# A mixture-of-experts kernel with a second model's context stream woven in: the order of the context's four branches

## The chip, the cores and the metric

The kernel runs on one core of a Trainium2 chip. A time is the device time of one execution in microseconds (us); the kernel before takes 1780.83 us, the median of three runs (1779.35 to 1781.1). Engines: PE (TensorE, matmuls), PEld (its weight loads), DVE (VectorE), ACT (ScalarE), POOL (GpSimd), SP (SyncE, which here only issues DMAs). Each engine works through its own instructions strictly in the order in which they were written into the program, and waits at semaphores for the others.

## The reference, cut to what matters

Two transformer blocks follow one another. The first ends in a mixture of experts: 256 tokens, 32 experts of three weight matrices each, two experts per token.

```python
def expert_block(args):
    xblk, e = args
    return (jax.nn.silu(xblk @ w1[e]) * (xblk @ w3[e])) @ w2[e]
```

The second block is a model of two layers over 256 latent tokens and 256 context tokens. In its first layer the context goes through the same four branches as the latents, then through a projection and a feed-forward part:

```python
yc_a = fourier_mix(pc[..., COL_FOURIER:COL_FOURIER + gw])
yc_b = dense_attention(heads(pc[..., COL_NA:COL_NA + gw]), na_kc, na_vc).reshape(bsz, -1, gw)
yc_c = spatial_gating(pc[..., COL_SGU:COL_SGU + 2 * gw], ...)
qc = heads(pc[..., COL_DIFF:COL_DIFF + gw])
oc_d = diff_attend(qc[..., :DIFF_QK_DIM], qc[..., DIFF_QK_DIM:], df_kc[..., :DIFF_QK_DIM], ...)
yc = jnp.concatenate([yc_a, yc_b, yc_c, yc_d], axis=-1) @ w_out[l]
cx = cx + cg1 * yc
cx = cx + cg2 * sq_relu_mlp(hc2, w_ff1[l], w_ff2[l])
```

The four branches read the same normalized context and write different columns of `yc`; none of them needs another. The context depends on nothing of the first block, so the kernel computes its first layer beside the experts.

## The kernel before, in words

**The experts.** `moe` (L1091) goes through 32 experts, e0 to e31, in groups of 4, 4, 8, 8, 8. At a group's start `gather` (L1003) picks the tokens of its experts with matmuls against a 0/1 matrix (`pm<-oh,xn`). For each expert `scatter_mat` (L1025) makes the matrix that puts results back: POOL copies `oh4`, PE transposes it (`pm<-ident,oh`, `pm<-wt,oh`). `expert` (L1040) then loads six pieces of weights, 1 MiB each (two halves of w1 and w3, two of w2), and does a chain of three matmul stages: 64 matmuls `pm<-w,xg` over w1 and w3; an eviction by ACT (`eh`) and two transposes on PE (`pm<-ident,eh`); the gated activation on ACT and DVE (`eth`, `ex`); 32 matmuls `pm<-w,ex` over w2; the weighting, split into a high and a low part (`yh`, `yl`); and 16 matmuls `acc<-yh,sc` and `acc<-yl,sc` that add the expert's result to four accumulators that stay in PSUM through all experts. Within one expert PE thus has three turns at which it waits for ACT and DVE, unless other matmuls stand in its order there: from `xg` to the transposes of `eh`, from these to `ex`, and from `ex` to `acc`.

**The side work.** The context's first layer is a Python generator, `context_side` (L1855), which calls `context_layer` (L1773), which calls `context_mixer` (L1545). Each `yield` ends a step. `moe` takes one step after each expert (`side()`, L1119; two go before e0 and one earlier still), so that step and expert stand side by side in the program. Its matmuls write `pf` tiles (two PSUM banks of their own, `ps_lin` and `ps`, L180 and L187). A linear layer is `lin` (L293): the weights (1 MiB pieces, `half`, L243) are split by ACT and DVE into a high and a low part (`wh`, `wl`), and each product takes three matmuls. Over 512 columns that is 96 matmuls with 256 moving columns (activations stationary or weights stationary by the job, `WJob`), or 48 with 512 (`TJob`). The feed-forward part, `ff_side` (L1686), has 16 steps that alternate between 96 `pf<-hh,wh` and the like (first layer) and 48 `pf<-wh,hh` and the like (second).

In `context_mixer` the steps of the kernel before are, by the expert that they follow: the neighbourhood branch (for the context a dense attention, `na`) two units each after e0 to e3; the query and key layer of the differential attention, W1, after e4; its attention, `diff`, two units each after e5 to e8, which loads no weights; W3 and the Fourier branch after e9; the gating unit (`sgu_v`, one piece w_su, `sgu`) after e10. Then `context_layer` goes on: the two halves of the output projection after e11 and e12 (`pf<-wh,yh` and the like), the norm after e13, the feed-forward part after e14 to e29.

**What sets the order.** The program's text is only the input: a scheduler with a timeline of its own puts the instructions of each engine into their final order, so that pieces of a step can stand ahead of pieces of the expert before it, and the reverse. SP's loads are ordered by it too. The 1 MiB pieces of experts and side work share ten buffers (`p16`, `p16x`): a load is issued when an earlier piece has been read. DVE, ACT and PE are shared by both streams.

Of the kernel before, what the change touches and what calls it, by code (L numbers as in the profile page):

```python
# [110 lines left out]
class Builder:  # L111
# [1433 lines left out]
    def context_mixer(self, lhs, kvc, kd_d, nlam, put):  # L1545

        W = self.a["w_in_2"][0]
        new = lambda s: self.t2([P, 2, 256], F32, s)
        nk, nv, dv, dk = kvc
        npad = self.head_pads(64)  # L1550
        self.lin(self.chunk(W[0]), 8, 512, [WJob(lhs, self.two_w(npad, nk))])
        yield
        self.lin(self.chunk(W[2]), 8, 512, [TJob(lhs, self.two_t(nv, dv))])
        yield
        yield from itertools.islice(self.in_turn(self.na(npad, [nk], [nv], None, put), 0), 1, None, 2)
        dpad = self.head_pads(32)
        self.lin(self.chunk(W[1]), 8, 512, [WJob(lhs, self.two_w(dpad, dk))])
        yield
        self.planes(dk, kd_d)
        df = self.diff(self.padded(dpad, [dk]), 2, [dv], nlam, 0, put)  # L1560
        yield from itertools.islice(self.in_turn(df, 0), 1, None, 2)
        fa, sv = new("fa"), new("sv")
        self.lin(self.chunk(W[3]), 8, 512, [TJob(lhs, self.two_t(fa, sv))])
        self.fourier(fa, put)
        yield
        self.sgu_v(sv, 0)
        su = new("su")
        self.lin(self.chunk(self.a["w_su_2"][0], (P, 2048)), 8, 256, [WJob(lhs, self.two_w(su, None))])
        self.sgu(su, sv, 0, put)
        yield  # L1570

    def mixer(self, l, lhs, kvc, kd_d, nlam, put, proj, late, w, held, fill):

# [537 lines left out]
```

## Time and profile before

| | |
|---|---|
| median of the timed runs | 1780.83 us (1779.35 to 1781.1) |
| the profiled execution | 1776.12 us, span 1774.3 us |
| PE / PEld busy | 1657.3 us (93%) / 1317.0 us (74%) |
| DVE / ACT / POOL busy | 961.2 us (54%) / 724.0 us (41%) / 61.6 us (3%) |
| DMA | 495.83 MB, mean 279 GB/s |
| the experts' weights | 192 pieces of 1 MiB, median 12.1 us from issue to landing |

The span holds one execution from its first to its last instruction; 1.8 us of the profiled execution lie around it. The experts take the stretch from some 455 us to 1073 us, in slices 11 to 25 of the page's second part. There PE and the DMA engines are both mostly at 9 tenths, so the share of the whole span says little: what a change is worth is read from the places inside the stretch where PE waits, and from what it waits for there. An idle time in square brackets in a timeline's row is that of the engine just before the row, with what ended it; "issue" means that the profile shows nothing that did.

### The profile page before, as it was taken

Reading aid. Unit: us, or ns where it says so; the run is one execution under the profiler, and the core shown is the slowest. Engines: PE = TensorE matmul, PEld = TensorE weight load, DVE = VectorE, ACT = ScalarE, POOL = GpSimd, SP = SyncE. Lnnn points to the kernel's source line nnn. Section 1 sums busy time; section 2 is a strip of 40 time slices with the busy share of each in tenths; the row PEclk is TensorE's granted clock in tenths of the full one; section 3 lists DMA queues with packets and bytes.
Section 4 is the critical chain, followed back from the end, with each engine's and each line's share of the span. In section 5 each row is a group of like instructions: output and inputs, shape, how many; then the busy total and the mean of one; then the engine's idle time right before and its main releaser. Section 6 shows DMA issues by size and latency. Waiting matters only on the chain.

```text
span 1774.3 us, 31435 instructions
## 1 busy us (share of the span) xinstructions
PE 1657.3 (93%) x13088; PEld 1317.0 (74%) x13088; DVE 961.2 (54%) x1719; ACT 724.0 (41%) x1257; POOL 61.6 (3%) x104
## 2 busy tenths in 40 slices
PE   4999999999888998999999997999999999899998
PEld 1678766667565556776677666878999998689998
DVE  5626556467223445544454457586545456766555
ACT  2414434343223433333233336565444445645443
POOL 0000000000000000000000001010000000100000
PEclk9899999999899999999999999999999999989999
DMA  9654588977699999989979997725877746245551
GB/s 372 278 211 169 199 317 310 345 278 265 240 420 420 421 395 407 379 365 420 416 318 401 421 394 268 232 81 172 291 253 264 263 165 208 76 130 188 192 190 43
DMA packets 79060, 495.83 MB, mean 279 GB/s; under 512 B 8928, under 2 KB 15744, under 8 KB 22464
## 3 DMA queue, kind: packets, MB, share of 16 engines
q1 hardware_dynamic: 74496, 478.30, 70.6%
q0 software_dynamic: 3152, 10.47, 2.0%
q10 hardware_dynamic: 1264, 4.98, 0.7%
q8 instruction: 105, 1.72, 0.4%
q14 instruction: 43, 0.35, 0.1%
HBM read 486.91 MB, written 6.82 MB: 278 GB/s over the span
## 4 chain that ended last, share of the span: by engine, by line
PE 64%; DVE 3%; DMA 3%; ACT 2%; issue 2%; POOL 0%; DVEq 0%; ACTq 0%; POOLq 0%
PE pf L200 23%; PE pm L200 19%; PE acc L200 11%; PE pa L200 5%; PE pj L200 3%; PE pm L203 1%; DMA w<-in_w_in 1%; PE pf L203 1%; DMA w<-in_e 1%; PE pada L200 1%; DVE wl L209 1%; DMA w<-in_w_out 1%; DVE sm L1337 1%; ACT e L206 0%; ACT wh L206 0%
## 5 line engine op out<-in xcount | busy, mean ns | idle before, releaser
L209 DVE TENSOR_TENSOR wl<-w,wh 128x1024 fp32r<-128x1024 f32 x346 | 422.4, 1225 | 385.4 <-PE pa L200 100.5
L206 ACT ACTIVATE wh<-w 128x1024 fp32r<-128x1024 f32 x346 | 362.8, 1059 | 407.1 <-PE pa L200 169.5
L200 PE MATMUL pf<-hh,wh 128*128 128x256 f32 x592 | 167.0, 284 | 4.6 <-ACT hh L206 2.4
L200 PE MATMUL pf<-hh,wl 128*128 128x256 f32 x592 | 164.4, 283 | 2.1 <-DVE wl L209 2.1
L200 PE MATMUL pf<-hl,wh 128*128 128x256 f32 x592 | 165.3, 281 | 0.5 <-DVE hl L209 0.5
L200 PE MATMUL acc<-hh,wh 128*128 128x256 f32 x512 | 143.5, 280 | 0.0
L200 PE MATMUL acc<-hl,wh 128*128 128x256 f32 x512 | 142.9, 279 | 0.0
L200 PE MATMUL acc<-hh,wl 128*128 128x256 f32 x512 | 142.9, 279 | 0.0
L200 PE MATMUL pm<-w,xg 128*32 128x256 f32 x2048 | 131.2, 387 | 2.7 <-ACT sm L206 1.8
L200 PEld LDWEIGHTS pf<-hh,wh 128*128 128x128 f32 x592 | 111.8, 189 | 9.8 <-ACT hh L206 3.1
L200 PEld LDWEIGHTS pf<-hh,wl 128*128 128x128 f32 x592 | 110.5, 189 | 5.0 <-DVE wl L209 2.8
L200 PEld LDWEIGHTS pf<-hl,wh 128*128 128x128 f32 x592 | 111.8, 189 | 1.5 <-DVE hl L209 0.9
L200 PEld LDWEIGHTS pm<-w,xg 128*32 128x32 f32 x2048 | 66.6, 111 | 50.9 <-issue 11.2
L200 PEld LDWEIGHTS acc<-hh,wh 128*128 128x128 f32 x512 | 96.4, 188 | 5.9 <-ACT wh L206 4.2
L200 PEld LDWEIGHTS acc<-hh,wl 128*128 128x128 f32 x512 | 96.8, 189 | 0.0
L200 PEld LDWEIGHTS acc<-hl,wh 128*128 128x128 f32 x512 | 96.4, 188 | 0.0
L200 PE MATMUL pada<-w,csil 128*32 128x512 f32 x576 | 83.7, 613 | 5.6 <-DMA w<-in_ada_w 5.6
L200 PE MATMUL pm<-w,ex 128*32 128x256 f32 x1024 | 63.6, 388 | 24.0 <-issue 22.3
L200 PE MATMUL pm<-hh,wh 128*128 128x256 f32 x256 | 71.7, 280 | 0.0
L200 PE MATMUL pm<-hl,wh 128*128 128x256 f32 x256 | 71.7, 280 | 0.0
L200 PE MATMUL pm<-hh,wl 128*128 128x256 f32 x256 | 71.5, 279 | 0.0
L200 PEld LDWEIGHTS pm<-w,ex 128*32 128x32 f32 x1024 | 33.8, 111 | 46.6 <-issue 28.9
(512 smaller groups left out, 3484.7 us busy)
## 6 DMA issues: line engine op xcount, KB each, us to landing
w<-in_e SPq DMA_DIRECT2D x192, 1024.0 KB, 12.1
w<-in_ff SPq DMA_DIRECT2D x96, 1024.0 KB, 5.6
w<-in_ada_w SPq DMA_DIRECT2D x72, 1024.0 KB, 7.1
w<-in_w_in SPq DMA_DIRECT2D x54, 1024.0 KB, 7.8
w<-in_w_out SPq DMA_DIRECT2D x16, 1024.0 KB, 7.0
w<-in_ret_w_o SPq DMA_DIRECT2D x4, 1024.0 KB, 5.2
w<-in_w_su SPq DMA_DIRECT2D x3, 1024.0 KB, 6.5
adab<-in_ada_b SPq DMA_DIRECT2D x9, 256.0 KB, 12.6
```

What stands on the lines that cost most here:

```text
L200: return self.nc.tensor.matmul(out, lhsT, rhs, start=start, stop=stop, skip_group_check=True)
L203: return self.nc.tensor.transpose(out, in_, self.ident)
L206: return self.nc.scalar.activation(out, in_, f, **k)
L209: return self.nc.vector.tensor_tensor(out, a, b, op=op)
L1337: self.nc.vector.tensor_reduce(mn, s, AX.X, ALU.min)
```

## The change

Within `context_mixer` two blocks of lines change places: W3, the Fourier branch and the gating unit now come straight after the neighbourhood branch, and the differential attention comes last. No instruction's operands change in size, and the number of steps stays 13.

```diff
         yield from itertools.islice(self.in_turn(self.na(npad, [nk], [nv], None, put), 0), 1, None, 2)
-        dpad = self.head_pads(32)
-        self.lin(self.chunk(W[1]), 8, 512, [WJob(lhs, self.two_w(dpad, dk))])
-        yield
-        self.planes(dk, kd_d)
-        df = self.diff(self.padded(dpad, [dk]), 2, [dv], nlam, 0, put)
-        yield from itertools.islice(self.in_turn(df, 0), 1, None, 2)
         fa, sv = new("fa"), new("sv")
         self.lin(self.chunk(W[3]), 8, 512, [TJob(lhs, self.two_t(fa, sv))])
         self.fourier(fa, put)
...
         self.sgu(su, sv, 0, put)
         yield
+        dpad = self.head_pads(32)
+        self.lin(self.chunk(W[1]), 8, 512, [WJob(lhs, self.two_w(dpad, dk))])
+        yield
+        self.planes(dk, kd_d)
+        df = self.diff(self.padded(dpad, [dk]), 2, [dv], nlam, 0, put)
+        yield from itertools.islice(self.in_turn(df, 0), 1, None, 2)
```

By steps: W3 with Fourier now follows e4 (was e9), the gating unit e5 (was e10), W1 e6 (was e4), and the differential attention e7 to e10 (was e5 to e8). From e11 on each step follows the same expert as before. The scheduler's order moves beyond that: it differs on PE, DVE and ACT from e4 up to e30, as the three places below show.

First place: PE where W1's linear layer begins (`hh` and `hl` are the normalized context there, `wh` and `wl` the split weights). Before, it follows at once on e4's transposes (`eh_4571`) and w2 stage (`ex`):

```order
L203 MATMUL pm_4573<-ident_81,eh_4571 128x128 x2
L200 MATMUL pm_4581<-w_4534,ex_862_4577 32x256 x8
L200 MATMUL pm_4581<-w_4536,ex_862_4577 32x256 x8
L200 MATMUL pf_4628<-hh_2818,wh_4630 128x256
L200 MATMUL pf_4628<-hl_2819,wh_4630 128x256
L200 MATMUL pf_4629<-hh_2818,wh_4630 128x256
L200 MATMUL pf_4629<-hl_2819,wh_4630 128x256
```

Now it stands behind the whole of e7's first stage (`xg` into `pm_5196`, its last two rows here) and the gating unit's matmuls (`sguw,sv`):

```order
L200 MATMUL pm_5196<-w_5188,xg_4488 32x256 x2
L200 MATMUL pm_5196<-w_5190,xg_4488 32x256 x2
L200 MATMUL pf_4924<-sguw_4919,sv_4621 64x128 x8
L200 MATMUL pf_5050<-hh_2818,wh_5052 128x256
L200 MATMUL pf_5050<-hl_2819,wh_5052 128x256
L200 MATMUL pf_5050<-hh_2818,wl_5053 128x256
L200 MATMUL pf_5050<-hh_2818,wh_5052 128x256
```

W1's step follows e6 in the program's text now, but its matmuls stand behind the next expert's first stage; before, they stood ahead of it.

Second place: PE at expert e15, in the feed-forward part (`pm_6736` is e15's first stage, `eh_6769` its eviction, `hh` and `hl` the hidden rows of the side work). Before, two side matmuls stand between `xg` and the transposes, and ten (six of them here) between the transposes and `ex`:

```order
L200 MATMUL pm_6736<-w_6730,xg_5270 32x256 x2
L200 MATMUL pf_6822<-wh_6824,hh_6583 128x512
L200 MATMUL pf_6823<-wh_6824,hh_6583 128x512
L203 MATMUL pm_6771<-ident_81,eh_6769 128x128 x2
L200 MATMUL pf_6822<-wl_6825,hh_6583 128x512
L200 MATMUL pf_6822<-wh_6824,hl_6584 128x512
L200 MATMUL pf_6823<-wl_6825,hh_6583 128x512
L200 MATMUL pf_6823<-wh_6824,hl_6584 128x512
```

Now both turns have nothing in them; side matmuls come after `ex` and a gather, two ahead of `acc`:

```order
L200 MATMUL pm_6736<-w_6730,xg_5343 32x256 x2
L203 MATMUL pm_6771<-ident_81,eh_6769 128x128 x2
L200 MATMUL pm_6779<-w_6732,ex_1315_6775 32x256 x8
L200 MATMUL pm_6779<-w_6734,ex_1315_6775 32x256 x8
L200 MATMUL pm_6906<-oh_6902,xn_3197 128x256 x4
L200 MATMUL pm_6913<-oh_6902,xn_3197 128x256 x4
L200 MATMUL pf_6822<-wh_6824,hh_6583 128x512
L200 MATMUL pf_6823<-wh_6824,hh_6583 128x512
L200 MATMUL acc_3891<-yh_6798,sc_6720 128x256
```

The twelve side matmuls that filled e15's two turns have moved behind its w2 stage.

Third place: PE at expert e26 (`eh_9142`), from the transposes on. Before, 39 side matmuls (the first five here) stand between `ex` and `acc`:

```order
L203 MATMUL pm_9144<-ident_81,eh_9142 128x128 x2
L200 MATMUL pm_9152<-w_9105,ex_1724_9148 32x256 x8
L200 MATMUL pm_9152<-w_9107,ex_1724_9148 32x256 x8
L200 MATMUL pf_9197<-hh_6417,wh_9199 128x256
L200 MATMUL pf_9197<-hl_6418,wh_9199 128x256
L200 MATMUL pf_9198<-hh_6417,wh_9199 128x256
L200 MATMUL pf_9198<-hl_6418,wh_9199 128x256
L200 MATMUL pf_9197<-hh_6417,wl_9200 128x256
```

Now there are four, and the accumulation (`acc_3891`) follows them:

```order
L203 MATMUL pm_9144<-ident_81,eh_9142 128x128 x2
L200 MATMUL pm_9152<-w_9105,ex_1724_9148 32x256 x8
L200 MATMUL pm_9152<-w_9107,ex_1724_9148 32x256 x8
L200 MATMUL pf_9197<-hh_6417,wh_9199 128x256
L200 MATMUL pf_9197<-hl_6418,wh_9199 128x256
L200 MATMUL pf_9198<-hh_6417,wh_9199 128x256
L200 MATMUL pf_9198<-hl_6418,wh_9199 128x256
L200 MATMUL acc_3891<-yh_9171,sc_9093 128x256
L200 MATMUL acc_3892<-yh_9171,sc_9093 128x256
```

Here the order of the first two turns is alike in both, and the third has lost all but four of its matmuls.

## Rows read from the trace of the kernel before

**Rows 1.** Stretches: length, busy us of the engines, PEclk, DMA share, GB/s

```profile
500.00:700.00 200.00, 177.07 (x1722) 118.77 (x1713) 79.62 (x196) 67.53 (x164) 6.33 (x14) 0.98 1.01 415
640.00:700.00 60.00, 52.33 (x486) 35.31 (x478) 29.10 (x58) 18.07 (x34) 2.97 (x6) 0.97 1.01 410
700.00:1060.00 360.00, 338.81 (x3308) 255.13 (x3312) 182.59 (x285) 116.98 (x205) 8.33 (x18) 1.00 0.95 388
700.00:760.00 60.00, 59.32 (x558) 43.10 (x558) 34.49 (x65) 24.14 (x42) 1.21 (x3) 0.98 0.86 341
880.00:940.00 60.00, 55.51 (x518) 44.38 (x520) 30.03 (x42) 19.62 (x32) 0.81 (x2) 1.00 0.83 329
```

**Rows 2.** ACT's timeline (start us, us): the evictions eh of e5, e6, e8, e9, e14, e31

```profile
540.35 0.39 ACT L206 ACTIVATE eh<-pm 128x256 f32<-128x256 f32 x1
...
553.26 0.38 ACT L206 ACTIVATE eh<-pm 128x256 f32<-128x256 f32 x1 [3.71 <-PE pm L200]
...
590.72 0.39 ACT L206 ACTIVATE eh<-pm 128x256 f32<-128x256 f32 x1 [0.53 <-PE pm L200]
...
605.21 0.39 ACT L206 ACTIVATE eh<-pm 128x256 f32<-128x256 f32 x1 [1.81 <-PE pm L200]
...
712.85 0.39 ACT L206 ACTIVATE eh<-pm 128x256 f32<-128x256 f32 x1 [0.32 <-PE pm L200]
...
1068.77 0.39 ACT L206 ACTIVATE eh<-pm 128x256 f32<-128x256 f32 x1 [0.39 <-PE pm L200]
```

**Rows 3.** What PE waited for, 701 to 1060 us: us in total, times, longest

```profile
PE pm L200 <- issue: 10.6, 10, 1.1
PE pm L203 <- ACT eh L206: 5.8, 11, 0.6
...
PE acc L200 <- ACT yh L206: 1.0, 2, 0.5
```

**Rows 4.** PE's timeline at e18, whose first two turns hold no side matmul

```profile
793.41 3.66 PE L200 MATMUL pm<-w,xg 128*32 128x256 f32 x64
797.60 0.44 PE L203 MATMUL pm<-ident,eh 128*128 128x128 f32 x2 [0.53 <-ACT eh L206]
799.10 1.93 PE L200 MATMUL pm<-w,ex 128*32 128x256 f32 x32 [1.06 <-issue]
```

**Rows 5.** PE's timeline at e16, with side matmuls around the transposes

```profile
762.70 0.28 PE L200 MATMUL pf<-hh,wl 128*128 128x256 f32 x1
762.82 0.38 PE L203 MATMUL pm<-ident,eh 128*128 128x128 f32 x2
762.96 0.36 PE L200 MATMUL pf<-hh,wh 128*128 128x256 f32 x1
```

**Rows 6.** PE's timeline at the third turn of e21, with two side matmuls in it

```profile
864.33 0.73 PE L200 MATMUL pf<-wh,hh 128*128 128x512 f32 x2
865.58 0.39 PE L200 MATMUL acc<-yh,sc 32*128 32x256 f32 x4 [0.52 <-ACT yh L206]
```

**Rows 7.** PE's timeline at e20: its first stage cut by side matmuls

```profile
825.74 0.62 PE L200 MATMUL pm<-w,xg 128*32 128x256 f32 x4
...
840.09 0.44 PE L203 MATMUL pm<-ident,eh 128*128 128x128 f32 x2 [0.48 <-ACT eh L206]
```

**Rows 8.** PE's timeline: a run of 24 side matmuls, from its start to the next

```profile
1039.19 0.73 PE L200 MATMUL pf<-wh,hh 128*128 128x512 f32 x2
...
1044.99 0.39 PE L200 MATMUL acc<-yh,sc 32*128 32x256 f32 x4
```

**Rows 9.** PE's timeline at e13's second turn

```profile
700.24 3.23 PE L200 MATMUL pm<-w,ex 128*32 128x256 f32 x32 [3.44 <-issue]
```

**Rows 10.** DVE's timeline just before: the context's residual and e13's gated activation

```profile
697.84 1.29 DVE L209 TENSOR_TENSOR cx<-cx,a 128x512 f32<-128x512 f32 x2
699.04 0.28 DVE L222 SCALAR_TENSOR_TENSOR ex<-eth,pm 128x128 f32<-128x128 f32 x1
```

**Rows 11.** SP's timeline at the store of the context's differential keys

```profile
541.21 0.33 SPq L225 DMA_DIRECT2D kd_d<-planes  x1
```

## The prediction

> **What bounds the kernel now.** I read three views in this order: the busy time by stretches, to see which resource is full where; the list of what PE waited for, to see what a PE wait consists of in the longer stretch; and the timelines of PE at single experts, for the price of each kind of wait.
>
> The stretches fall into two [rows 1]. From 500 to 700 us, in which the moved steps lie, the DMA share is 1.01 at 415 GB/s: weights arrive without a pause, and a piece of 1 MiB (1.049 MB) takes 1.049 / 0.415 = 2.5 us. The change moves no byte out of this stretch, so it can't end much earlier. PE is busy for 177.1 of 200 us there. From 700 to 1060 us, the feed-forward steps after e14 to e29, the share is 0.95, with 0.86 and 0.83 in two of its parts, so the DMA engines have pauses: buffers weren't free because PE hadn't read them. PE sets the pace: from e14's eviction at 712.85 to e31's at 1068.77 [rows 2] there are 355.9 us, 20.9 an expert, where eight pieces need 20.0. Of 360 us PE is idle for 21.2, and the list of waits says what these are [rows 3]: 10 waits of 1.06 us ahead of `ex`, 11 of 0.53 ahead of the transposes of `eh`, 2 of 0.5 ahead of `acc`; together 17.4 us. No wait for a DMA is among them. They are the turns inside an expert. At e18 [rows 4] nothing of the side work stands in the first two turns, and PE pays 0.53 and 1.06. At e16 [rows 5] side matmuls stand there and the next one starts 0.12 us after the last: the turn costs nothing. So in the second stretch time hangs on the place of side matmuls within PE's order, and that order has changed there too.
>
> **The change part by part.**
>
> The steps themselves: same instructions, same shapes, same count of steps, same bytes. Work: 0.
>
> The first stretch, moved steps. W1's matmuls now stand behind e7's first stage. Its weights are asked for ahead of e7's, so e7's first four pieces land six pieces, 6 x 2.5 = 15 us, after e6's last one. In between PE has e6's second stage (1.93 us [rows 4]), its three turns (some 3 us) and its own short matmuls (some 2 us), then e7's 3.66 us: it stands idle for about 15 - 11 = 4, say 5 us, with W1's weights already there. What makes it good: the four steps of the differential attention bring no weights. An expert there takes PE 553.26 - 540.35 = 12.9 us or 605.21 - 590.72 = 14.5 us [rows 2], mean 13.7, and its six pieces take 15.0. So PE gains 1.3 us on the DMA in each, 5 us in four. From e11 on both kernels load the same pieces in the same order, and I take this part at 0. Bounds: +5 if nothing is made good; below, PE's whole idle time from 640 to 700 us, 60 - 52.3 = 7.7 us [rows 1], if it all went.
>
> The store of the differential keys sits in SP's queue behind 20 weight loads now, 12 before. Before, SP issued it at 541.21 [rows 11], in a stretch in which the DMA share is 1.01 [rows 1]; a later store is covered by the same loads. The gating unit's small loads wait in POOL's queue behind earlier `oh4` copies, and e7's copy now waits behind them; what needs it is `acc` at the far end of e7. Both: 0; if that cover is gone, the price is one late `acc`, some 3 us, inside the 5 above.
>
> e13's second turn. Before, PE waits 3.44 us ahead of `ex` [rows 9], because DVE works off the context's residual (`cx`, until 699.1) and only then the activation at 699.04 [rows 10]. The last 22 projection matmuls stand behind e13's first stage before and ahead of it now, so the residual starts about 3.7 us earlier (64 `xg` matmuls [rows 4]) and is out of DVE's way; transposes of the normalized context then stand in that turn. Between 0 and -3.4 us; I take -3, the residual's DVE time being shorter than the lead.
>
> The second stretch, e14 to e30, counted from PE's order, with prices from rows:
> - transposes of `eh` with nothing ahead of them: 11 before, 15 now (all but e16 and e24). 4 x 0.53 [rows 4] = +2.1
> - `ex` with nothing between it and the transposes: 10 before, 15 now. 5 x 1.06 [rows 4] = +5.3
> - `acc` with only two 512-column or four 256-column matmuls ahead of it: 2 before (e21, e22), 8 now (e14, e18, e19, e20, e21, e26, e27, e29). 6 x 0.5 [rows 6] = +3.0
> - first stages cut open by side matmuls: 9 cuts before (e20, e22, e28, e30), 14 now (e18, e20, e22, e26, e28, e30). At e20, three cuts, the stage takes from 825.74 to 840.09, 14.35 us [rows 7]. In it lie 64 `xg` (3.66 us), 36 side matmuls at (1044.99 - 1039.19) / 24 = 0.242 us [rows 8], 8.7 us, and the first turn, 0.53. That leaves 1.45, 0.5 a cut. 5 x 0.5 = +2.5
>
> Together +12.9. Bounds: 0, if the DMA takes over the pace, and +16, if each gap also delays the split of the side weights.
>
> Sum: 0 - 3 + 12.9 = +9.9, in round numbers +10. Made against the profiled execution (1776.1 us: span 1774.3, 1.8 around it) this is 1786. The median of the timed runs lies 4.7 above that execution, and the change moves both alike: 1780.8 + 10 = **1791 us**.
>
> **A rule weighed against it.** The first stretch goes from weight-heavy and weight-free steps in turn (after e4 two pieces, four steps with none, then 2, 1, 2, 2) to three heavy steps, four without, two heavy. The rows say that the DMA share is 1.01 through all of it [rows 1]. The Trainium skill, Perfetto Trace Analysis, section Optimization Strategy, says that a kernel with regimes bound by different engines may gain from interleaving them; the new order puts heavy steps together, so by that rule it speaks against the change. By the row the sum has 0 there, by the rule it would be the +5 of e7's wait, a result that stands among the rivals.
>
> **The rivals.**
>
> *Faster.* The weights pace the second stretch after all, and PE's new gaps lie in time in which it would have waited for pieces: then only the first part's gain counts. For it: a DMA share of 0.95, and just 0.9 us between PE's 20.9 and the DMA's 20.0 us an expert. Against: no wait of PE for a DMA in the list [rows 3], and 0.86 and 0.83 in two parts [rows 1]. It decides from the point at which PE needs under 20.0 us an expert. Time: 1780.8 - 3 = 1778, or 1775 if part of the 7.7 us goes as well.
>
> *No change that can be told.* The gain in the first stretch is at its bound (-7.7 with e13's wait in it) and the gaps cost little over half, +8, since a wait that falls earlier lets DVE and ACT split side weights ahead, which saves waits elsewhere. For it: PE's idle time from 640 to 700 us [rows 1] and the DVE wait of e13 [rows 9], which show that the side work's chain can run late. Against: the turns are latencies of a chain that no other work shortens. Time: 1781.
>
> *Slower still.* e7's wait isn't made good, and the rest comes as counted: 1791 + 5 = 1796, up to 1799 with the upper bound of the second stretch. For it: 1.3 us a step is the difference of two near numbers. Against: from e11 on both orders wait for the same pieces, so the weights come no later.
>
> *That the new order isn't what runs* is no rival: the scheduler's order is fixed before the program runs.
>
> **How the numbers follow.** Forecast 0.58, slower still 0.16, no change 0.16, faster 0.10. 0.2% is 3.6 us here, about what a measurement can tell from no change. The forecast's own range is 1785 to 1797 (each term at half and at one and a half of its size, less what cancels); the range for 8 in 10 reaches to 1780 and 1799, so that it takes in most of no change and slower still, and leaves out the faster case. Slower: 0.58 + 0.16 = 0.74; within: the 0.16 of no change and 0.02 of the faster case, whose 1778 lies inside the bound; faster: the other 0.08.
>
> **What would show it.** In the profile after, from e14 to e31: the time between the evictions of `eh` should be about 369 us against 355.9; waits ahead of `ex` of 1.06 us some 15 times, ahead of the transposes 0.53 us some 15 times, ahead of `acc` eight times; the DMA share below 0.95. From 500 to 700 us the DMA share should stay at 1.0, with a wait ahead of e7's first stage of about 5 us, and e14's eviction come at 710 us, 0 to 5 us ahead of 712.85. The forecast is wrong if PE waits for weights after e14, if the turns cost less with less side work in them, or if e14 comes over 5 us late.

## The result and the profile after

The changed kernel takes 1803.97 us (median of four runs, 1800.97 to 1805.64) against 1780.96 us: ratio 1.0125, interval 1.0109 to 1.0140, 23 us slower. The forecast was slower by 10, 1791 in a range of 1780 to 1799. The direction was right, and so was the account of the stretch from e14 to e31; the size was not.

First the stretches of the kernel after, columns as in [rows 1], with two parts more:

```profile
500.00:700.00 200.00, 176.10 (x1718) 118.52 (x1714) 78.05 (x191) 65.11 (x160) 6.78 (x14) 0.98 0.99 405
700.00:1060.00 360.00, 329.90 (x3203) 244.88 (x3196) 171.60 (x262) 113.56 (x198) 7.15 (x17) 1.00 0.92 376
760.00:820.00 60.00, 56.13 (x562) 41.54 (x561) 28.28 (x39) 18.48 (x31) 1.20 (x3) 1.00 0.91 372
820.00:880.00 60.00, 53.74 (x548) 40.24 (x547) 25.43 (x37) 17.06 (x31) 1.20 (x3) 1.00 0.92 372
```

The same two parts in the kernel before:

```profile
760.00:820.00 60.00, 56.82 (x614) 45.06 (x614) 27.64 (x41) 19.12 (x35) 1.58 (x3) 1.00 1.01 418
820.00:880.00 60.00, 56.12 (x510) 40.53 (x503) 29.86 (x40) 16.73 (x28) 1.21 (x3) 1.00 1.01 418
```

The first stretch, cut at fixed times, looks as before (177.1 us of PE, share 1.01); what lies inside it is taken up further down. In the second, PE does less in the same 360 us (338.8 before) and the DMA share falls from 0.95 to 0.92. The two short parts show more: before, the weights came without a pause from 760 to 880 us; now there are pauses. What PE waited for from 701 to 1060 us, after (compare [rows 3]):

```profile
PE pm L200 <- issue: 14.8, 14, 1.1
PE pm L203 <- ACT eh L206: 7.9, 15, 0.6
PE acc L200 <- ACT yh L206: 4.3, 8, 0.8
```

These are the three turns: 4.2, 2.1 and 3.3 us more than before. The evictions of e14 and e31 (compare [rows 2]):

```profile
719.14 0.38 ACT L206 ACTIVATE eh<-pm 128x256 f32<-128x256 f32 x1 [1.26 <-PE pm L200]
...
1089.66 0.38 ACT L206 ACTIVATE eh<-pm 128x256 f32<-128x256 f32 x1 [1.15 <-PE pm L200]
```

From the one to the other it is 370.5 us, before 355.9: +14.6. The forecast for this was 369. But e14 comes at 719.14, 6.3 us later than before, where the forecast had 710 and called over 5 us late a sign of being wrong. The next table places the rest, for all kernels, in us between evictions of `eh` (one profiled execution each; up to e4's eviction it is 517 to 522 us, in the sixth experiment 532).

| kernel | e4 to e11 | e11 to e14 | e14 to e31 | e31 to the end | timed ratio to before |
|---|---|---|---|---|---|
| before | 130.7 | 64.0 | 355.9 | 705.5 | 1 |
| after | 126.6 | 71.0 | 370.5 | 709.5 | 1.0125 |
| 1: new branches, late order of before | 130.0 | 69.0 | 355.6 | 703.0 | 1.0023 |
| 2: old branches, late order of after | 131.2 | 68.4 | 370.8 | 712.3 | 1.0119 |
| 3: after, turns filled | 130.1 | 67.4 | 374.0 | 720.0 | 1.0206 |
| 4: before, turns filled | 130.9 | 66.2 | 356.3 | 720.9 | 1.0094 |
| 5, 12: before, whole groups | 132.2, 129.4 | 66.4, 63.3 | 353.9, 352.3 | 706.1, 705.7 | 0.9953, 0.9943 |
| 6: differential first | 112.7 | 68.4 | 360.1 | 712.9 | 1.0046 |
| 7: before, turns emptied | 131.0 | 66.4 | 377.6 | 709.7 | 1.0123 |
| 8: gating unit last, late order of before | 130.3 | 60.7 | 361.3 | 708.3 | 1.0019 |
| 9: new branches, whole groups | 130.0 | 68.9 | 353.7 | 705.5 | 0.9999 |
| 10: gating unit last | 130.8 | 58.8 | 366.8 | 712.0 | 1.0066 |
| 11: gating unit last, whole groups | 130.5 | 60.5 | 353.2 | 706.6 | 0.9958 |

### The profile page after: what moved, and what is told of

It is laid out like the page before. It is cut to its first block, busy times and chain, and to the rows that moved or that the text cites. A ratio compares the mean times of both kernels' runs of the same rounds, so it can differ in the third digit from the quotient of the medians.

```text
span 1799.2 us, 31445 instructions
## 1 busy us (share of the span) xinstructions
PE 1672.7 (93%) x13088; PEld 1322.6 (74%) x13088; DVE 963.5 (54%) x1719; ACT 721.2 (40%) x1257; POOL 60.9 (3%) x104
## 4 chain that ended last, share of the span: by engine, by line
PE 64%; DVE 3%; DMA 3%; ACT 2%; issue 2%; SPq 0%; DVEq 0%; ACTq 0%
PE pf L200 23%; PE pm L200 19%; PE acc L200 11%; PE pa L200 4%; PE pj L200 3%; PE pm L203 1%; DMA w<-in_w_out 1%; DVE wl L209 1%; PE pf L203 1%; PE pada L200 1%; DMA w<-in_e 1%; DMA k_d<-planes 0%; DVE sm L1337 0%; ACT e L206 0%; ACT eh L206 0%
## 5 line engine op out<-in xcount | busy, mean ns | idle before, releaser
L200 PE MATMUL pm<-w,xg 128*32 128x256 f32 x2048 | 135.3, 388 | 4.0 <-DMA w<-in_e 2.9
L200 PEld LDWEIGHTS pm<-w,ex 128*32 128x32 f32 x1024 | 34.7, 110 | 44.7 <-issue 30.0
```

The lines of the kernel that those rows point to most:

```text
L200: return self.nc.tensor.matmul(out, lhsT, rhs, start=start, stop=stop, skip_group_check=True)
```

## Experiments

**1 and 2: late order and branch order apart.** The instructions from e14's scatter matrix to e31's accumulation are the same in both kernels; only their order on the engines differs. So each kernel can be given the other's late order, by edges that fix the order on one engine and add no wait. `ROWS` is a table of instruction numbers in the wanted order, one line each for PE, DVE and ACT.

```diff
-            gains = self.moe(x, side, *routed)
+            gains = self.moe(x, side, *routed); in_order(self, ROWS)
...
+                i = at[f"I-{x}"]
...
+                if last is not None:
+                    b.tc.add_manual_dep(i, last.name, no, reason="order")
+                last = i
```

Expected of the first:

> The changed branch order, but from e14 to e31 PE, DVE and ACT keep the order that the kernel before has there. Theory 1 (the late order's uncovered turns are most of the loss): e14's to e31's eviction comes back from 370.5 us to 355 to 358, the time falls by about 14.6, from 1804 to 1789; what is left, some 8 us over the kernel before, comes from e4 to e14 and from outside the experts. Rival (the branch order itself costs the time, by the place of the weight loads, and the late order only shows it): 370 us stay, 1802 to 1806.

Of the second:

> The reverse: the branch order of the kernel before, with the changed kernel's order of PE, DVE and ACT from e14 to e31. Theory 1: e14 to e31 takes about 370 us instead of 356, the time is 1781 + 14.6 = 1795.6. Rival (the branch order itself): 356 us and 1781.

Measured: 1784.03 against 1779.62 us (1.0023, 1.0011 to 1.0034), and 1801.14 (1.0119, 1.0098 to 1.0140). PE's waits in the first, 701 to 1060 us:

```profile
PE pm L200 <- issue: 10.6, 10, 1.1
PE pm L203 <- ACT eh L206: 5.8, 11, 0.6
PE pf L200 <- DVE wl L209: 1.6, 3, 1.1
PE pf L203 <- DVE xn L218: 1.4, 2, 0.8
PE acc L200 <- ACT yh L206: 1.0, 2, 0.5
```

The turns' waits are those of before to a tenth, and e14 to e31 takes 355.6 us, with the new branch order in front of it. With the old branches and the new late order it takes 370.8. So the loss sits in the late order: some 21 us of the 23, of which 14.9 lie between e14 and e31. The branch order by itself costs 4. The rival is out. Theory 1 was too high for the first (1789 for 1784) and too low for the second (1795.6 for 1801.1): it left 8 us to the early part and gave the late order only the 14.6 between e14 and e31.

**3 and 4: fill the turns.** PE's order from e14 to e31, edited so that every turn holds side matmuls, held back from those just ahead. At e19 of the kernel before, counted in program instructions:

```diff
-67 side | xg | transposes | ex | 12 side | acc
+52 side | xg | 5 side | transposes | 10 side | ex | 12 side | acc
```

Expected, for the changed kernel and for the one before:

> The changed kernel with PE's order edited from e14 to e31 so that every turn has side matmuls in it: 0.6 us between xg and the transposes, 1.2 us before ex, 1.3 us before acc, taken from those just ahead. By the order the uncovered part of the turns falls from 32.1 us to 1.7. Theory 1: e14 to e31 falls from 370.5 to between 342 (where 17 experts of 20.0 us stand by the weight loads) and 352, the time to between 1775 and 1786. Rival (the weight loads set the pace and the turns only fill their time): 368 to 371 us, 1801 to 1805.

> The kernel before with the same edit: the uncovered part falls from 22.3 us to 0.3. Theory 1: e14 to e31 falls from 355.9 to between 341 and 348, the time from 1781 to between 1766 and 1773. Rival (the loads already set the pace, at a share of 0.95): 354 to 356, 1779 to 1782.

Measured: 1815.27 (1.0206, 1.0187 to 1.0226) and 1795.91 (1.0094, 1.0077 to 1.0112). Both slower, where theory 1 had them faster, by 18 to 29 us and by 8 to 15. e14 to e31 takes 374.0 and 356.3 us: the fourth is where its rival had it, and most of its loss stands after e31. What PE waited for in the fourth, 715 to 1060 us:

```profile
PE pf L200 <- ACT wh L206: 10.4, 5, 3.0
PE pf L200 <- DVE wl L209: 5.1, 5, 1.5
PE pf L200 <- DVE a L209: 1.2, 1, 1.2
```

The turns are gone from the list, and waits of the side matmuls for their split weights stand there, 16.7 us together for the 17.4 of [rows 3]. PE's timeline at e19 of that kernel shows one of them, and ACT's what it was doing:

```profile
822.38 1.93 PE L200 MATMUL pm<-w,ex 128*32 128x256 f32 x32
827.31 0.73 PE L200 MATMUL pf<-wh,hh 128*128 128x512 f32 x2 [3.00 <-ACT wh L206]
```

```profile
821.78 1.30 ACT L206 ACTIVATE a<-pf 128x512 f32<-128x512 f32 x2 [0.19 <-PE pf L200]
823.13 1.33 ACT L206 ACTIVATE hh<-a 128x512 fp32r<-128x512 f32 x2
825.89 0.42 ACT L206 ACTIVATE yh<-ey 128x256 fp32r<-128x256 f32 x1 [1.43 <-DVE ey L222]
826.22 2.94 ACT L206 ACTIVATE wh<-w 128x1024 fp32r<-128x1024 f32 x3
```

Held back, the last 15 matmuls of a side step end in the second turn; only then does ACT get the step's result (821.78), turn it into `hh`, and split the next weights (826.22); PE stands still for 3 us. Part of that is ACT's order, which stayed as it was: it has `yh` ahead of `wh`, and ACT idles 1.43 us for DVE before it. The side steps also end later: after e31 there are 720.9 us left, not 705.5, with 9.3 us of waiting for the context's last norm (`xn`). And the wait is followed by a dip of the clock:

```profile
820.00:828.00 8.00, 5.00 (x59) 3.28 (x51) 5.08 (x9) 5.22 (x9) 0.40 (x1) 1.00 1.01 420
828.00:832.00 4.00, 3.47 (x9) 2.75 (x9) 1.65 (x2) 1.15 (x2) 0.00 (x0) 0.57 1.01 420
```

So it is with the waits of 2.31 us at 873 (clock 0.62 from 871 to 880) and 3.00 us at 1006 (0.76 from 1005 to 1012). From e14's to e31's eviction, the kernel before, the fourth and (for later) the seventh experiment:

```profile
712.85:1068.77 355.92, 334.30 (x3276) 252.79 (x3276) 179.43 (x272) 114.41 (x201) 8.80 (x18) 1.00 0.96 391
716.91:1073.25 356.34, 338.04 (x3251) 252.83 (x3252) 165.68 (x236) 109.11 (x190) 7.67 (x17) 0.98 0.94 386
716.68:1094.26 377.58, 342.83 (x3279) 257.27 (x3279) 181.51 (x273) 118.92 (x203) 7.89 (x18) 0.98 0.92 370
```

In the fourth PE is idle 3.3 us less than before (18.3 for 21.6) and busy 3.7 us more, at a lower clock: what the filled turns saved is gone again within the stretch.

So theory 1, that the bare time of the turns is a sum that any side matmul can pay, has fallen. New theory (2): a turn's cover helps if it consists of whole groups, the 12 or 24 matmuls of one split, and a step's end isn't delayed.

**5 and 12: whole groups.** In the kernel before, e16 and e17 have such an order by themselves. It was given to e18 to e23 and e26 to e29 (PE's order alone is fixed). At e18:

```diff
-xg | transposes | ex | 29 side | acc | 67 side
+xg | 23 side | transposes | 33 side | ex | 29 side | acc | 11 side
```

> The kernel before, PE's order edited from e18 to e23 and e26 to e29: these experts get the pattern that e16 and e17 have already, whole groups of side matmuls in the turns (24, 33 and 29 at an even expert, 12, 12 and 24 at an odd one), no first stage cut, each side step done within its expert. The uncovered part of the turns falls from 22.3 us to 5.2. e17, e18, e25 and e26, which come right behind the pattern in the kernel before, take 18.3 to 18.7 us there, others 20 to 23. Theory 2 (a turn's cover is worth its price if it is made of whole groups, so that no split of weights waits for a part of one): e14 to e31 falls from 355.9 us to between 330 and 342, the time from 1780 to between 1758 and 1768. Rival (PE's idle time is given by something else and only moves from place to place, as in the run before): 354 to 358 us, 1779 to 1795.

> The fifth experiment's kernel once more, beside x11 on one chip and beside the same runs of the kernel before: 1772, ratio 0.995. If its gain was that chip's, the ratio is within 0.998 to 1.002.

Measured: 1772.12 (0.9953, 0.9936 to 0.9969) and, on another chip, 1768.97 (0.9943, 0.9925 to 0.9961): faster than both kernels, by less than expected. e14 to e31 takes 353.9 and 352.3 us, where theory 2 had 330 to 342 and the rival 354 to 358: in this stretch the rival was right. PE's waits, and ACT's timeline at e18 in the fifth:

```profile
PE pf L200 <- ACT wh L206: 11.9, 8, 1.5
PE pf L200 <- DVE wl L209: 4.2, 8, 0.5
```

```profile
796.40 0.17 ACT L206 ACTIVATE sm<-pm 128x1 f32<-128x1 f32 x1
799.72 0.38 ACT L206 ACTIVATE eh<-pm 128x256 f32<-128x256 f32 x1 [3.15 <-PE pm L200]
800.00 1.99 ACT L206 ACTIVATE wh<-w 128x1024 fp32r<-128x1024 f32 x2
```

Again the waits moved, now to a step's first split, which ACT's order puts behind `eh`; ACT itself idles 3.15 us ahead of that `eh`. An order of ACT and DVE made to fit the new one of PE wasn't tried, so that theory 2 fell with the old order of ACT is all that is shown. The clock takes its part here as well: 0.98 from e14 to e31 in the fifth, 1.00 before. The DMA share is 1.01 from 780 to 840 us, as in the kernel before from 760 to 880. That the loads set the pace there isn't shown: from 715 to 1060 us no engine's list of waits holds a load in the kernel before, and in the fifth only ACT's does, with 0.5 us. The profiled pairs can't show where the gain of 8 to 11 us lies: the fifth's profiled execution (1777.43) is the slowest of its six, and that of the kernel before (1776.12) lies 2 to 5 us below its medians.

**6: another branch order.**

```diff
-neighbourhood | W1, differential | W3, Fourier | gating unit
+W1, differential | neighbourhood | W3, Fourier | gating unit
```

> Another branch order: differential attention, neighbourhood, W3 and Fourier, gating unit. The scheduler's order leaves 17.6 us of turns uncovered from e14 to e31 (kernel before 22.3, changed kernel 32.1). Theory 1 (this number sets the time of e14 to e31: 9.8 us of it went with 14.6 in the changed kernel): 4.7 x 1.5 = 7 us less, e14 to e31 takes 349, the time is about 1773 if the first stretch is unchanged. Rival (the place of the differential attention, last or not, sets it): as the kernel before, 356 and 1780.

Measured: 1787.97 (1.0046, 1.0030 to 1.0063). A miss: 360.1 us for 349. The turns' waits fell as counted, from 17.4 to 12.5 us in the lists, but those of side matmuls for their splits rose by as much, from 1.6 to 5.6 (715 to 1060 us), and PE is busy 5.0 us longer (339.3 for 334.3). Fewer bare turns than in the kernel before bring nothing by themselves; the count leaves out what PE waits for instead.

**7: empty the turns.** The side matmuls of the first two turns at e14 to e17, e24 and e25 stand behind `ex`. At e16:

```diff
-xg | 23 side | transposes | 33 side | ex | 29 side | acc
+xg | transposes | ex | 85 side | acc
```

> The kernel before with the reverse edit at e14 to e17, e24 and e25: all side matmuls of the first two turns stand behind ex, in whole groups; nothing else moves. Uncovered turns rise by 9.2 us (22.3 to 31.5), close to the changed kernel's 32.1. Theory 1: e14 to e31 rises by 9 to 14 us, to 365 to 370, the time to 1789 to 1794. Rival (idle time only moves): 356 us, 1779 to 1782.

Measured: 1802.63 (1.0123, 1.0103 to 1.0143), the changed kernel's time, with old branches. e14 to e31 takes 377.6 us, more than the 365 to 370 expected. PE at e16 shows the two waits that weren't there in [rows 5]; the third row is from e21. The list is that from 701 to 1060 us:

```profile
769.99 0.44 PE L203 MATMUL pm<-ident,eh 128*128 128x128 f32 x2 [0.53 <-ACT eh L206]
771.49 1.93 PE L200 MATMUL pm<-w,ex 128*32 128x256 f32 x32 [1.06 <-issue]
...
876.61 3.19 PE L200 MATMUL pm<-w,ex 128*32 128x256 f32 x32 [2.33 <-issue]
```

```profile
PE pm L200 <- issue: 22.8, 16, 3.4
PE pm L203 <- ACT eh L206: 7.2, 12, 1.4
```

The longest wait in the list, 3.4 us, is that of [rows 9] at e13 and no bare turn. By the stretches shown with the fourth, PE is idle 13.1 us longer than before from e14 to e31 (34.7 for 21.6) and busy 8.5 us longer with nearly the same matmuls, at a clock of 0.98: behind the wait of 2.33 us the w2 stage takes 3.19 us instead of 1.93. That wait is at e21, which wasn't edited, so the loss spreads; ACT, too, now waits 36.9 us for side weights (715 to 1060 us), before not at all. So bare turns alone, put where the kernel before has cover, do cost time, and more than the 9.2 us counted, since other waits follow and the longer ones cost clock as well. In the changed kernel no wait in this stretch was long enough for that (1.1 us at most, clock 1.00); that both kernels come out near 1803 us is chance, 21.7 us from e14 to e31 here and 14.6 there. Together with 3 to 6: taking cover away loses time; adding it moved PE's waits, and paid only in whole groups, and little.

**8 and 10: is it that the differential attention stands last?** The gating unit last; in 8 with the late order of before, in 10 with the scheduler's own.

```diff
-neighbourhood | W3, Fourier | gating unit | W1, differential
+neighbourhood | W3, Fourier | W1, differential | gating unit
```

> Branch order: neighbourhood, W3 and Fourier, differential attention, gating unit last; from e14 to e31 PE, DVE and ACT in the order of the kernel before. Against the first experiment only the gating unit and the differential attention have changed places. Theory 3 (with the differential attention last, its chain of scores, softmax and transposes stands bare in front of the output projection, which needs all of y): e11's to e14's eviction, 68 to 71 us with the differential attention last and 64 to 68 with the gating unit last, goes back to about 66, the time from 1784 to 1780. Rival (the order of the branches costs by something else, as by the late load of W1's weights at e7): 1784.

> The branch order of x8 with the order that the scheduler gives it late: 25.8 us of turns uncovered (kernel before 22.3, changed kernel 32.1). Theory 2, with the loads as a floor (uncovered time costs only beyond what the loads hide, which the kernel before about uses up): 3.5 x 1.5 = 5 us more from e14 to e31, 361 us, the time 1785. Rival (the count says nothing, the differential attention's place late in the order does): 370 and 1800.

Measured in 8: 1782.44 (1.0019, 1.0004 to 1.0033). e11 to e14 fell to 60.7 us, further than expected, but the time didn't follow: e15 took 26.5 us instead of 20.9, and PE waits 1.82 us for the context's norm there. The experts ran ahead and the side steps didn't. Between 1784 and 1782 the two theories can't be told apart by the time, so what the differential attention costs by standing last stays open. In 10: 1789.20 (1.0066, 1.0050 to 1.0081), 366.8 us for 361: between the kernels before and after, as its count is, at twice the price expected.

**9 and 11: whole groups with other branches.**

> The changed kernel's branch order with the late order of the fifth experiment (whole groups in the turns). If the late order is nearly all of the loss: e14 to e31 takes 352 to 356 us, the DMA share is 1.0 from 780 to 900 us, and the time is that experiment's 1772 plus the 4 us of the first one, 1776. Rival (a third of the loss is the early part's): 1780 or more.

> The branch order of x8 (gating unit last), which brings e14's eviction at 709 us, 7 us ahead of the branch order before (716), with the late order of the fifth experiment. If those 7 us are an expert's lead that the side steps don't share, they are given back at e15 (26.5 us there in x8 instead of 20.9), and the time is 1770 to 1773, as the fifth experiment's 1772. Rival (the lead stays, since the turns no longer pace the stretch): 1765.

Measured in 9: 1779.43 (0.9999, 0.9987 to 1.0011), nearer the rival's 1780 than 1776, though e14 to e31 takes 353.7 us as expected: the branch order seems to cost more here (7 us against 5) than the 4 of the first experiment. With this late order the changed branch order is as fast as the kernel before; by the ratios (1.0125 and 0.9999) 22 us of the changed kernel's time went with the order of PE from e14 on. One of its parts, where the changed kernel had a DMA share of 0.92 (from 760 to 820 us it is 0.92 here too):

```profile
820.00:880.00 60.00, 56.01 (x549) 42.44 (x549) 31.56 (x44) 20.52 (x35) 1.21 (x3) 0.97 1.01 420
```

In 11: 1772.76 (0.9958, 0.9941 to 0.9975), as expected of a lead that is given back: e11 to e14 takes 60.5 us, and e15 26.4.

## Why the prediction was wrong, step by step

- *Moved steps, work 0; first stretch 0.* The work was right, the 0 was not. The table's e4 to e11 got shorter (126.6 to 130.1 us with the new branches: after, 1, 3, 9; 129.4 to 132.2 with the old: before, 2, 4, 5, 7, 12), but only because work moved behind e11's eviction: PE is busy 7.4 us less ahead of it and 8.1 us more from there to e14. PE's idle time grew. From e4 to e11 and from e11 to e14, first before, then after:

```profile
518.18:648.85 130.67, 117.09 (x1172) 77.76 (x1172) 54.52 (x153) 48.65 (x126) 3.36 (x8) 0.99 1.01 414
648.85:712.85 64.00, 55.74 (x493) 35.98 (x494) 32.52 (x64) 22.71 (x42) 2.97 (x6) 0.95 0.99 396
```

```profile
521.54:648.14 126.60, 109.68 (x1151) 74.35 (x1151) 49.70 (x123) 43.40 (x108) 5.26 (x11) 1.00 1.00 408
648.14:719.14 71.00, 63.80 (x518) 39.31 (x518) 36.75 (x93) 26.08 (x60) 1.85 (x3) 0.95 0.94 383
```

  From e4 to e11 PE idles 13.6 us before and 16.9 after (12.4 to 13.6 and 15.3 to 17.0 in the kernels named). The wait ahead of e7's first stage is in it, 2.9 us in two pieces and not 5:

```profile
573.15 0.63 PE L200 MATMUL pm<-w,xg 128*32 128x256 f32 x4 [1.12 <-DMA w<-in_e]
575.50 1.92 PE L200 MATMUL pm<-w,xg 128*32 128x256 f32 x28 [1.73 <-DMA w<-in_e]
```

  So "made good" failed: 3.3 us more of idle time stand where the sum had 0. By the rule that the prediction took from the Trainium skill, Perfetto Trace Analysis, section Optimization Strategy (regimes bound by different engines may gain from being interleaved), it would have had +5 here; the trace lies between the two.
- *e13's second turn, −3.* This step failed too. The wait of [rows 9] did go; at e13 `ex` now follows without one. But from e11 to e14 PE's idle time fell only from 8.3 us to 7.2 (8.3 to 9.5 and 7.1 to 7.2 in the others), since other waits came two experts earlier. PE's timeline from e11's second turn on, after:

```profile
650.84 0.44 PE L203 MATMUL pf<-ident,a 128*128 128x128 f32 x2 [1.82 <-DVE a L222]
...
659.50 0.51 PE L203 MATMUL pf<-ident,a 128*128 128x128 f32 x2 [2.18 <-DVE a L222]
...
705.09 1.93 PE L200 MATMUL pm<-w,ex 128*32 128x256 f32 x32
```

  These are transposes of the differential attention, waiting for its softmax. The projection needs all of `y`, and its first matmul comes 24.1 us after e11's eviction (648.14 to 672.19), before 18.0 (648.85 to 666.84). Asking what is late next stopped at e13's own turn. The two terms together, e4 to e14: 0 − 3 was forecast, and the mean goes from 196.7 us (192.7 to 199.6 with the old branches) to 198.3 (197.5 to 199.0 with the new), +1.6. That is some 4.6 us of the miss, known no better than these spreads allow.
- *The second stretch, +12.9.* Right: +14.6, of which 8.6 are idle time of PE and 6.0 busy time. By term, in PE's waits from 701 to 1060 us: transposes 2.1 (forecast 2.1), `ex` 4.2 (5.3), `acc` 3.3 (3.0). Cut first stages: adding up PE's timeline from e14's to e30's eviction, the `xg` stages take 64.8 us in 30 pieces against 61.5 in 25, so 3.3 (forecast 2.5). Cuts of the accumulation, which had no term, take 13.7 against 11.9: 1.8 more. Together 14.7, a ledger of one execution.
- *After e31.* The sum had nothing there, and gave no reason. With the changed kernel's late order (after, 2) it is 709.5 and 712.3 us to the end; with that of before or of the fifth experiment 703.0 to 708.3 (before, 1, 5, 8, 9, 11, 12): +4 to 6. From e31's eviction to the end, before and after:

```profile
1068.77:1774.30 705.53, 671.33 (x5222) 616.40 (x5222) 425.67 (x714) 359.55 (x573) 32.44 (x40) 0.98 0.56 187
1089.66:1799.20 709.54, 675.36 (x5222) 619.18 (x5222) 427.48 (x715) 358.93 (x574) 32.41 (x40) 0.97 0.56 185
```

  PE is idle for 34.2 us in both; the 4.0 us are busy time of the same 5222 matmuls at a lower clock. Most of it stands right behind the experts: from 1060 to 1120 us the granted clock is 0.89, before from 1040 to 1100 it is 0.94, a loss of about 6.6 and 3.6 us. Whether the late order does this or the execution isn't settled: the eighth experiment, with the order of before, is at 708.3.
- *The rivals.* "Slower still" came nearest to the time; its reason (e7's wait isn't made good) is right for some 3 of its 5 us. "Faster" had half a point: the DMA engines are full in the kernel before at 760 to 880 us, which the mean of 0.95 hid. But no engine waits for a load there, and in the changed kernel PE's gaps cost in full.

With −3 taken as +1.6, the second stretch as 14.6, and 5 after e31, the sum is 21.2; measured 23.0. The rest isn't placed; e4's eviction comes 2.4 us later in the mean with the new branches (521.0 for 518.6), although the orders differ only from e4 on. Experiment 1 puts the branch order at 4 us, experiment 9 against 5 at 7 (1779.4 and 1772.1, runs of two chips), so that this part is known to some 3 us.

## What to carry to other kernels

A change of order in a program that a scheduler arranges is priced at the places where the arrangement differs, however far from the edit: here some 20 of 23 us lay behind e14, in steps that the edit doesn't touch, and could be moved from kernel to kernel by fixing the order alone. Count which short turns of a chain lose their cover, but price an added cover only after asking what PE will wait for instead: here the splits, whose order on ACT stayed as it was, and after the longer of these waits a lower clock. When work moves across the mark between two stretches, compare idle time, not length. When a branch with a long chain becomes the last before a join, look for its waits right in front of the join.

## What the runs showed of the hardware

PE's waits of up to 1.1 us, ten of them in the kernel before from 701 to 1060 us, left the granted clock at 1.00 over each part from 760 us on. After a wait of 3.00 us (experiment 4) it fell to 0.57 over the next 4 us, that is to the level of 1.2 GHz for most of it; after 1.47 and 0.53 us with a few matmuls between (experiment 5, at 799 to 802 us) to 0.68 over 5 us:

```profile
801.00:806.00 5.00, 4.37 (x23) 4.17 (x23) 2.36 (x2) 2.06 (x3) 0.00 (x0) 0.68 1.02 424
```

So the one wait of 3 us cost, by an estimate from these rows, 0.43 x 4 = 1.7 us on top, which waits of 1 us that stood apart didn't. Over a whole stretch it adds up: in experiment 7, with waits of up to 2.33 us from e14 to e31, the clock of 0.98 goes with 8.5 us more of busy time for nearly the same matmuls.
